# Two transformer blocks on one core: weight splits run further ahead, a late scaling moved, a bias moved from TensorE to VectorE, and a reordered latent head

## The chip, the cores and the metric

The kernel runs on one core of a Trainium2 chip, as one launch. The metric is the device time in microseconds (us), lower is better. The engines of the core that matter are TensorE (PE, matmuls; PEld is its weight load), VectorE (DVE), ScalarE (ACT), GpSimd (POOL) and the queue of SyncE (SP), which issues the transfers. Each engine has a list of instructions of its own; semaphores hold an instruction back until what it reads is there.

## The reference

Two blocks of two layers each work on 256 tokens of width 1024, in 32-bit floats. The first block (gated linear attention, a dense feed-forward and a mixture of eight experts) is not touched by the change. The second block has, for each of its two layers `i`, a feed-forward, an attention, a second feed-forward and a gated embedding:

```
for i in range(2):
    if i == 1: k_nope, k_rope, v = shared_kv(x, ...)
    x = post_norm(x, 0.5 * swiglu(x, ffn1_w_in[i], ffn1_w_out[i]), g0, b0)
    mix = fox_mixer(x, ...) if i == 0 else mla_mixer(x, ..., k_nope, k_rope, v)
    x = post_norm(x, mix, g1, b1)
    x = post_norm(x, 0.5 * swiglu(x, ffn2_w_in[i], ffn2_w_out[i]), g2, b2)
    gate = sigmoid(x @ ple_w_gate[i] + ple_b_gate[i])
    x = post_norm(x, gate * (p[i] @ ple_w_proj[i]), g3, b3)

swiglu(x)         = (silu(x @ w_gate) * (x @ w_up)) @ w_out      # 1024 -> 2816 -> 1024
post_norm(x, d)   = layer_norm(sqrt(2) * x + d) * g + b
mla_mixer: c_q    = rms_norm(x @ w_dq) * q_norm                   # 1024 -> 384, the "latent"
           q      = c_q @ w_uq ; keys and values from the shared latent of shared_kv
```

## The kernel before, in words

The 256 tokens are two tiles, t = 0 and 1, of 128 tokens (partitions) and 1024 columns. A product of 32-bit floats is made of three matmuls: each operand is split into a high part and a low part, and `mm3` (L304 to L311) adds high·high (L309), high·low and low·high (L310, L311) in one PSUM bank. The input of a stage is held turned round as `uh` and `ul` (high and low). The weights are split on the chip as well.

**The splitting of weights.** `want` queues the parts of the weights in the order in which they are used, a unit being a 128 x 2048 part of 1 MB that SP fetches into one of four `raw` buffers, and a half being 128 x 1024 of it. `emit(n)` splits the next n halves: a copy on ACT makes `wh` (L274), a subtraction on DVE makes `wl` (L275). At most `SLOTS` = 10 halves are live; a half gives its slot back when the last matmul that reads it has been written down, and a half of which a slot is not free is not begun. `tick(n)` calls `emit(n)` at fixed places of the program; where a stage has a string in the table `TICKS`, the digits of that string replace n until they are used up (the two first feed-forwards, `ffa0` and `ffa1`, have strings of 16 and 14 digits, the two second ones, `ffb0` and `ffb1`, none). `take(n)` hands units to a product and splits at once what is missing of them. The order in which instructions are written down is the order in which each engine runs them.

**The norm.** For each half of 512 columns, DVE adds the residual (`r`, L111) and takes statistics (L123); then `fin` makes `ve` (L331) on DVE and `rs` on POOL. `scale_all` makes x with two DVE operations per half (L149, L151); `apply` turns x round: eight PE transposes (L344), ACT writes `uh`, DVE `ul` (L361). The norm of tile 0 is done while the stage's last product of tile 1 runs. The two steps of tile 1 are put in the list `pend`; the next stage calls `nxt()` in the middle of its first products, and each call runs one of them.

**Feed-forward (`ffn`, L522).** The 2816 columns are 11 chunks j of 256. Chunks 0 and 1 go by token tile. From j = 2 on, `gate_up_T` (L449) makes two gates of 48 matmuls (i = 0, 1), each followed by ACT's `sg` (L468), DVE's `h` (L470) and the split of h in `fh` (ACT) and `fl` (DVE, L316), and by a product `down` of the chunk before (12 matmuls of 512 columns into `acc`). Each j uses six halves: four of gate and up, two of down. At the end come down(1, 9-1), down(0, 10), its norm, down(1, 9) and down(1, 10).

**Gated embedding (`ple`, L1747).** Four gates of 24 matmuls in the order (tile, half of columns) = (0,0), (0,1), (1,0), (1,1). The gate's bias is a row of 1024 numbers; it is fetched to one partition (`br`), split in `bh` and `bl`, and two matmuls with a contraction of one (L1775, L1776) add it to each gate in PSUM. Then ACT takes the sigmoid from PSUM, and DVE multiplies with the projection `pp` (L1792). `opened` runs in the middle of gate (0,0), `nxt` in the middle of gate (0,1).

**Latent attention (`mla`, L1546).** `down_q(t)` makes the latent of tile t (24 matmuls of 384 columns); its norm `cn` (L1480) goes over ACT, DVE and POOL, and then PE turns it round (L1487) and DVE and ACT split it (`cqh`, `cql`, L1492). `val` and `keys` make the values and keys of a pair of heads from the shared latent.

**Stages in the trace (us).** ffa0 about 1296 to 1512, forgetting attention (`fox`) 1516 to 1660, ffb0 1660 to 1852, ple0 1852 to 1894, shared_kv and ffa1 1894 to 2093, mla 2093 to 2270, ffb1 2270 to 2467, ple1 2467 to 2517. All before 1296 belongs to the first block.

Of the kernel before, what the change touches and what calls it, by code (L numbers as in the profile page):

```python
# [9 lines left out]
F32 = mybir.dt.float32  # L10
F32R = mybir.dt.float32r
BF16 = mybir.dt.bfloat16
AF = mybir.ActivationFunctionType
ALU = mybir.AluOpType
# [3 lines left out]
P = 128  # L18
D = 1024
S = 256  # L20
KB = D // P
# [26 lines left out]
ROW_LNB = 8  # L48
ROW_ADAG = 24
ROW_PLEB = 28  # L50
# [118 lines left out]
class Kern:  # L169
# [279 lines left out]
    def gate_up_T(self, wg, i, scale, pool, free, mid=None):  # L449

        nc = self.nc
        ps = self.pgu.tile([P, 512], F32, tag="gu", name="gu")
        for kb in range(KB):
            u, hf = wg[kb // 4], (kb % 4) // 2
            wh, wl = u.halves[hf]
            for g in range(2):
                o = (kb % 2) * 512 + g * CW + i * P

                self.mm3(ps[:, g * S:(g + 1) * S], wh[:, o:o + P], wl[:, o:o + P], self.uh[:, kb, :], self.ul[:, kb, :],
                         kb == 0 and g == 0, kb == KB - 1 and g == 1)  # L460
            if free and kb % 2:
                u.free(hf)
            if kb == 3:
                if mid:
                    mid()
                self.tick(self.rate)
        sg = self.acp.tile([P, CW], F32, name="sg")
        nc.scalar.activation(out=sg, in_=ps[:, :S], func=AF.Silu)  # L468
        h = self.acp.tile([P, S + 2], F32, tag="h", name="h")[:, :S]
        nc.vector.scalar_tensor_tensor(out=h, in0=sg, scalar=scale, in1=ps[:, S:], op0=ALU.mult, op1=ALU.mult)  # L470
        self.tick(self.rate)
        hh = pool.tile([P, S], F32R, name="fh", bufs=6)
        hl = pool.tile([P, S], F32R, name="fl", bufs=6)
        self.split(hh, hl, h)
        return hh, hl
# [46 lines left out]
    def ffn(self, name, scale, done, hook=None, early=None):  # L522


        wg, wd, h, hT, acc = {}, {}, {}, {}, {}
        n = NCH - 1

        def turn(s):
            hT[s] = self.parts_of(self.turn(h.pop(s)))

        def part(t, j):
            if j < 2:
                return hT.pop((t, j))
            return lambda i: tuple(z[:, t * P:(t + 1) * P] for z in hT[j, i])

        def down(t, j, norm=None, mid=None):
            if j not in wd:
                wd[j] = self.take()
            if j == 0:
                acc[t] = self.acc2()  # L540
            self.down(part(t, j), wd[j], acc[t], j == 0, j == n, t == 1, norm, mid)

        prev = None
        for i, (t, j) in enumerate([(0, 0), (0, 1), (1, 0), (1, 1)]):
            if hook and t == 0:
                hook(j)
            if i in (1, 2) and early:
                early(i)
            if j not in wg:
                wg[j] = self.take(2)  # L550

            def mid():
                if prev:
                    turn(prev)
                if i < 2:
                    self.nxt()
                if i == 0:
                    self.open_pool(name)
            ts = slice(t * P, t * P + P)
            h[t, j] = self.gate_up(lambda kb: self.uh[:, kb, ts], lambda kb: self.ul[:, kb, ts], wg[j], scale, t == 1,  # L560
                                   mid)
            if prev:
                down(*prev)
            prev = t, j
        for j in range(2, n + 1):
            if hook:
                hook(j)
            wg[j] = self.take(2)
            for i in range(2):
                first = (j, i) == (2, 0)  # L570
                hT[j, i] = self.gate_up_T(wg[j], i, scale, self.mp, i == 1, (lambda: turn(prev)) if first else None)
                if first:
                    down(*prev)

                elif j > 2 and not (i == 1 and j >= n - 1):
                    down(i, j - 1)
        down(1, n - 2)
        n0, n1 = done(0, acc[0]), done(1, acc[1])
        down(0, n, n0)
        n0.scale_all()  # L580
        down(1, n - 1)
        down(1, n, n1, n0.apply)
        self.close_pool()
        self.pend.extend([n1.scale_all, n1.apply])


    def proj_tok(self, ps, t, units, kbs=range(KB), free=False, mid=None, width=512, last=True):

        ts = slice(t * P, t * P + P)
        for kb in kbs:  # L590
            u, hf = units[kb // 4], (kb % 4) // 2
            wh, wl = u.halves[hf]
            sl = slice((kb % 2) * width, (kb % 2) * width + width)
            self.mm3(ps[:, :width], self.uh[:, kb, ts], self.ul[:, kb, ts], wh[:, sl], wl[:, sl], kb == 0,
                     last and kb == KB - 1)
            if free and kb % 2:
                u.free(hf)
            if kb == 3 and mid:
                mid()
            if kb % (2 if free else 4) == (1 if free else 3):  # L600
                self.tick()
# [238 lines left out]
    def out_rest(self, uo, y, kbs, done, acc):  # L840
        n0 = done(0, acc)
        n0.stats()
        n0.scale_all()
        acc = self.acc2()
        self.out_proj(uo, y(1), acc, kbs, True, True, True, {4: n0.apply}, 5)
        n1 = done(1, acc)
        n1.stats()
        self.pend.extend([n1.scale_all, n1.apply])

    def gla_turn(self, kout, st):  # L850

# [694 lines left out]
    def mla(self, done, row):  # L1546
        nc, tc, a = self.nc, self.tc, self.a
        scale = 192.0 ** -0.5
        c = {}
# [17 lines left out]
        def down_q(t, mid=None):  # L1567
            ps = self.pgu.tile([P, 512], F32, tag="gu", name="gu")
            self.proj_tok(ps, t, ud, free=t == 1, width=384, mid=mid)
            return self.rms_T(ps[:, :384], 384, COL_QN, c["cqh"], c["cql"], t)  # L1570
# [109 lines left out]
        self.nxt()  # L1680
        kn[0] = keys(kv)
        self.tick(0)
        kv, us[1] = self.take(2)
        v[1] = val(kv)
        f0()
        self.tick(0)
        f1 = down_q(1)
        self.rows(row)
        kn[1] = keys(kv)
        self.tick(0)  # L1690
        f1()
        qr[0], rest = rope(uq)
        qn[0] = queries(uq)
        rest()
# [40 lines left out]
                n0.apply()  # L1735
        n1 = done(1, acc[1])
        n1.stats()
        self.pend.extend([n1.scale_all, n1.apply])
        self.close_pool()


# [5 lines left out]
    def ple(self, i, done, row):  # L1747
        nc, a = self.nc, self.a
        c = {}

        def opened():
            self.nxt()
            self.open_pool(f"ple{i}")
            mp = self.mp
            pT = mp.tile([P, 2 * S], F32, name="pT")
            nc.sync.dma_start(out=pT, in_=a["ple_p"][i])
            ph = c["ph"] = mp.tile([P, 2 * S], F32R, name="ph")
            pl = c["pl"] = mp.tile([P, 2 * S], F32R, name="pl")
            self.split(ph, pl, pT)
            br = mp.tile([1, D], F32, tag="delta", bufs=2, name="br")  # L1760
            nc.sync.dma_start(out=br, in_=a["rows"][ROW_PLEB + i:ROW_PLEB + i + 1, :])
            bh = c["bh"] = mp.tile([1, D], F32R, name="bh")
            bl = c["bl"] = mp.tile([1, D], F32R, name="bl")
            self.split(bh, bl, br)
            one = c["one"] = mp.tile([1, P], F32R, name="one")
            nc.scalar.copy(one, self.onesf[:1, :])

        ug = self.take(4)
        d = {}

        def gate(t, hf, mid=None):
            ps = self.pgu.tile([P, 512], F32, tag="gu", name="gu")
            self.proj_tok(ps, t, ug[2 * hf:2 * hf + 2], free=t == 1, mid=mid, last=False)
            sl = slice(hf * 512, hf * 512 + 512)
            nc.tensor.matmul(ps, c["one"], c["bh"][:, sl], start=False, stop=False)  # L1775
            nc.tensor.matmul(ps, c["one"], c["bl"][:, sl], start=False, stop=True)  # L1776
            if t not in d:
                d[t] = self.mp.tile([P, D], F32, tag="delta", name="delta", bufs=2)
            nc.scalar.activation(out=d[t][:, sl], in_=ps, func=AF.Sigmoid)

        def emb(t, hf):
            sl = slice(hf * 512, hf * 512 + 512)
# [23 lines left out]
        for hf in range(2):  # L1806
# [4 lines left out]
            times(1, hf, pp[hf])  # L1811
            norms[1].stat(hf)
        norms[1].fin()
        self.close_pool()
        self.pend.extend([norms[1].scale_all, norms[1].apply])


    def load_ahead(self, *tiles):
# [196 lines left out]
    def second(self, layers=range(2)):  # L2015
        def norm(i, mode="T"):
            return lambda t, ps: Norm(self, t, ps, None, mode=mode)

        def rows_at(i):
            return lambda j: self.rows(ROW_LNB + 2 * i) if j == 3 else None  # L2020
        for l in layers:
# [17 lines left out]
            if self.stop == n + 1:  # L2039
                return self.dump()  # L2040
            self.phase(f"ffb{l}")
            self.ffn(f"ffb{l}", 0.5, norm(i + 2), rows_at(i + 2))
            if self.stop == n + 2:
                return self.dump()
            self.phase(f"ple{l}")
# [141 lines left out]
```

## Time and profile before

| what | value |
| --- | --- |
| time, median of 3 runs | 2522.14 us (2520.14 to 2528.19) |
| profiled execution: time, span | 2518.69 us, 2517.0 us |
| mean granted TensorE clock | 0.982 |
| PE busy | 2401.0 us (95%) |
| DVE busy | 1795.2 us (71%) |
| ACT busy | 1306.9 us (52%) |
| POOL busy | 46.7 us (2%) |
| DMA, mean | 238 GB/s |

PE is busy for 95% of the span, so that all its idle time is 116 us. A row of the timeline gives the start, the length, the engine, the line, the operation, what it writes and reads, and in brackets the idle time before it on its engine with the instruction that ended it. A matmul's length as shown overlaps the next one; the distance of two starts tells what one costs. PEclk is the clock that TensorE was granted, as a share of its 2.4 GHz level.

### The profile page before, as it was taken

To read this page: it belongs to the slowest core of one execution; us is meant where nothing else is said; L and a number is where in the kernel's file an instruction comes from. 1 tells how busy PE (TensorE), PEld (TensorE's weight loads), DVE (VectorE), ACT (ScalarE), POOL (GpSimd) and SP (SyncE) were. 2 spreads that over 40 slices of the span, in tenths; PEclk is the share of its full clock that TensorE was granted. 3 is DMA by queue.
4 is the path that set the end of the run, shared out by engine and by line. 5 is a ranking of instruction groups with operands and counts; after the bars stand their busy time and mean duration, and the time that the engine had idled before them with its cause. 6 is when DMAs were issued, how large, how long until landed. Compare 5 with 4: busy or idle time off the path is not lost. (4 is left out here: it accounts for less than half of the span.)

```text
span 2517.0 us, 34411 instructions
## 1 busy us (share of the span) xinstructions
PE 2401.0 (95%) x13608; PEld 2018.2 (80%) x13608; DVE 1795.2 (71%) x2587; ACT 1306.9 (52%) x1949; POOL 46.7 (2%) x79
## 2 busy tenths in 40 slices
PE   8999989899999999999979999999989998999997
PEld 5769978588788888888858887879968997878995
DVE  6876886699899999999984456655476556546546
ACT  3344443287777777777743345534434444443432
POOL 0000000000000000000000000000000001000000
PEclk9999999899999999999989999999999999999998
DMA  9756957479899999999855444335545544334551
GB/s 357 296 201 256 355 209 287 151 269 370 325 356 367 344 347 373 348 348 363 339 227 197 176 164 170 116 141 190 188 172 190 183 173 155 113 117 152 184 201 55
DMA packets 88925, 599.45 MB, mean 238 GB/s; under 512 B 10259, under 2 KB 11571, under 8 KB 20533
## 3 DMA queue, kind: packets, MB, share of 16 engines
q1 hardware_dynamic: 88756, 597.19, 63.3%
q8 instruction: 108, 1.77, 0.3%
q14 instruction: 61, 0.49, 0.1%
HBM read 596.10 MB, written 1.05 MB: 237 GB/s over the span
## 5 line engine op out<-in xcount | busy, mean ns | idle before, releaser
L275 DVE TENSOR_TENSOR wl<-raw,wh 128x1024 fp32r<-128x1024 f32 (+3 forms) x997 | 1162.4, 1208 | 124.5 <-ACT wh L274 120.1
L274 ACT CAST wh<-raw 128x1024 fp32r<-128x1024 f32 (+3 forms) x997 | 987.2, 1040 | 78.9 <-DMA raw<-in_moe_gu_dram 18.9
L309 PE MATMUL gu<-uh,wh 128*128 128x256 f32 (+1 forms) x1784 | 504.3, 283 | 0.6 <-ACT cc L784 0.6
L311 PE MATMUL gu<-uh,wl 128*128 128x256 f32 (+1 forms) x1784 | 501.5, 281 | 3.1 <-DVE wl L275 3.1
L310 PE MATMUL gu<-ul,wh 128*128 128x256 f32 (+1 forms) x1784 | 500.5, 281 | 0.0
L309 PEld LDWEIGHTS gu<-uh,wh 128*128 128x128 f32 (+1 forms) x1784 | 335.1, 188 | 6.8 <-issue 1.2
L310 PEld LDWEIGHTS gu<-ul,wh 128*128 128x128 f32 (+1 forms) x1784 | 335.3, 188 | 4.5 <-issue 0.3
L311 PEld LDWEIGHTS gu<-uh,wl 128*128 128x128 f32 (+1 forms) x1784 | 335.7, 188 | 3.8 <-DVE wl L275 3.3
L309 PE MATMUL gu<-wh,xs 128*128 128x512 f32 x704 | 280.8, 399 | 0.6 <-PEq L1285 0.6
L311 PE MATMUL gu<-wh,xs 128*128 128x512 f32 x704 | 277.2, 394 | 0.0
L310 PE MATMUL gu<-wl,xs 128*128 128x512 f32 x704 | 276.2, 392 | 0.0
L468 ACT ACTIVATE sg<-gu 128x256 f32<-128x256 f32 x90 | 34.7, 385 | 404.8 <-PE gu L311 404.8
L470 DVE SCALAR_TENSOR_TENSOR h<-sg,gu 128x256 f32<-128x256 f32 x90 | 37.9, 421 | 279.5 <-ACT sg L468 279.5
L310 PE MATMUL acc<-wl,hh 128*128 128x512 f32 x432 | 171.2, 396 | 2.6 <-DVE wl L275 2.6
L311 PE MATMUL acc<-wh,hl 128*128 128x512 f32 x432 | 170.5, 395 | 1.7 <-DVE hl L316 1.6
L309 PE MATMUL acc<-wh,hh 128*128 128x512 f32 x432 | 170.9, 396 | 0.5 <-ACT hh L315 0.5
L311 PEld LDWEIGHTS gu<-wh,xs 128*128 128x128 f32 x704 | 132.3, 188 | 29.4
L309 PEld LDWEIGHTS gu<-wh,xs 128*128 128x128 f32 x704 | 132.5, 188 | 26.7 <-DVE h L445 1.0
L310 PEld LDWEIGHTS gu<-wl,xs 128*128 128x128 f32 x704 | 132.6, 188 | 26.3
L310 PE MATMUL acc<-wl,fh 128*128 128x512 f32 x360 | 142.7, 396 | 8.3 <-DVE wl L275 8.3
L309 PE MATMUL acc<-wh,fh 128*128 128x512 f32 x360 | 144.0, 400 | 1.0
L315 ACT CAST hh<-trh 128x256 fp32r<-128x256 f32 x108 | 40.3, 373 | 195.9 <-PE trh L481 195.8
(394 smaller groups left out, 3399.3 us busy)
## 6 DMA issues: line engine op xcount, KB each, us to landing
raw<-in_moe_gu_dram SPq DMA_DIRECT2D x175, 1024.0 KB, 5.5
raw<-in_ffn_gu_dram SPq DMA_DIRECT2D x110, 1024.0 KB, 4.8
raw<-in_moe_dn_dram SPq DMA_DIRECT2D x87, 1024.0 KB, 5.0
raw<-in_ffn_dn_dram SPq DMA_DIRECT2D x55, 1024.0 KB, 4.9
raw<-in_ada_w_dram SPq DMA_DIRECT2D x48, 1024.0 KB, 5.1
raw<-in_w_in_dram SPq DMA_DIRECT2D x24, 1024.0 KB, 5.9
raw<-in_fox_in_dram SPq DMA_DIRECT2D x12, 1024.0 KB, 5.1
ww<-in_w_out_dram SPq DMA_DIRECT2D x16, 512.0 KB, 7.9
```

What stands on the lines that cost most here:

```text
L274: nc.scalar.copy(wh[:, :f], r)
L275: nc.vector.tensor_tensor(out=wl[:, :f], in0=r, in1=wh[:, :f].bitcast(F32), op=ALU.subtract)
L309: mm(out, xh, yh, start=first, stop=False)
L310: mm(out, xh, yl, start=False, stop=False)
L311: mm(out, xl, yh, start=False, stop=last)
L315: self.nc.scalar.copy(h, src)
L468: nc.scalar.activation(out=sg, in_=ps[:, :S], func=AF.Silu)
L470: nc.vector.scalar_tensor_tensor(out=h, in0=sg, scalar=scale, in1=ps[:, S:], op0=ALU.mult, op1=ALU.mult)
```

## The change

Five edits. (1) In `gate_up_T` both calls of `tick` offer two halves instead of one (`self.rate` is 1 in the second block and 2 in the first). (2) The scaling of tile 1, `n1.scale_all`, is written at the end of its own stage instead of in the next one's first product; `None` keeps its place in `pend`. This is done in `ffn`, `out_rest` (the end of the linear and the forgetting attention), `mla` and `ple`. (3) The bias of the gated embedding is fetched as 128 equal rows (`pleb`, 512 KB) in chunk 4 of the feed-forward before it; DVE adds it to the gate from PSUM into `delta`, and ACT takes the sigmoid in place. The two matmuls per gate, the split of the bias row and its transfer are gone. (4) The rows of the norm are still fetched at chunk 3, by the new hook. (5) In `mla` the second tile's latent product `down_q(1)` comes before `val(1)` instead of behind it, and the second turn (`f1`) comes before `keys(1)` instead of behind it.

```diff
--- before.py
+++ after.py
@@ -463,12 +463,12 @@
             if kb == 3:
                 if mid:
                     mid()
-                self.tick(self.rate)
+                self.tick(2)
         sg = self.acp.tile([P, CW], F32, name="sg")
         nc.scalar.activation(out=sg, in_=ps[:, :S], func=AF.Silu)
         h = self.acp.tile([P, S + 2], F32, tag="h", name="h")[:, :S]
         nc.vector.scalar_tensor_tensor(out=h, in0=sg, scalar=scale, in1=ps[:, S:], op0=ALU.mult, op1=ALU.mult)
-        self.tick(self.rate)
+        self.tick(2)
         hh = pool.tile([P, S], F32R, name="fh", bufs=6)
         hl = pool.tile([P, S], F32R, name="fl", bufs=6)
         self.split(hh, hl, h)
@@ -580,11 +580,12 @@
         n0.scale_all()
         down(1, n - 1)
         down(1, n, n1, n0.apply)
+        n1.scale_all()
         self.close_pool()
-        self.pend.extend([n1.scale_all, n1.apply])
-
-
-    def proj_tok(self, ps, t, units, kbs=range(KB), free=False, mid=None, width=512, last=True):
+        self.pend.extend([None, n1.apply])
+
+
+    def proj_tok(self, ps, t, units, kbs=range(KB), free=False, mid=None, width=512):
 
         ts = slice(t * P, t * P + P)
         for kb in kbs:
@@ -592,7 +593,7 @@
             wh, wl = u.halves[hf]
             sl = slice((kb % 2) * width, (kb % 2) * width + width)
             self.mm3(ps[:, :width], self.uh[:, kb, ts], self.ul[:, kb, ts], wh[:, sl], wl[:, sl], kb == 0,
-                     last and kb == KB - 1)
+                     kb == KB - 1)
             if free and kb % 2:
                 u.free(hf)
             if kb == 3 and mid:
@@ -845,7 +846,8 @@
         self.out_proj(uo, y(1), acc, kbs, True, True, True, {4: n0.apply}, 5)
         n1 = done(1, acc)
         n1.stats()
-        self.pend.extend([n1.scale_all, n1.apply])
+        n1.scale_all()
+        self.pend.extend([None, n1.apply])
 
     def gla_turn(self, kout, st):
 
@@ -1680,15 +1682,15 @@
         self.nxt()
         kn[0] = keys(kv)
         self.tick(0)
+        f1 = down_q(1)
+        f0()
+        self.rows(row)
         kv, us[1] = self.take(2)
         v[1] = val(kv)
-        f0()
         self.tick(0)
-        f1 = down_q(1)
-        self.rows(row)
+        f1()
         kn[1] = keys(kv)
         self.tick(0)
-        f1()
         qr[0], rest = rope(uq)
         qn[0] = queries(uq)
         rest()
@@ -1735,7 +1737,8 @@
                 n0.apply()
         n1 = done(1, acc[1])
         n1.stats()
-        self.pend.extend([n1.scale_all, n1.apply])
+        n1.scale_all()
+        self.pend.extend([None, n1.apply])
         self.close_pool()
 
 
@@ -1757,26 +1760,18 @@
             ph = c["ph"] = mp.tile([P, 2 * S], F32R, name="ph")
             pl = c["pl"] = mp.tile([P, 2 * S], F32R, name="pl")
             self.split(ph, pl, pT)
-            br = mp.tile([1, D], F32, tag="delta", bufs=2, name="br")
-            nc.sync.dma_start(out=br, in_=a["rows"][ROW_PLEB + i:ROW_PLEB + i + 1, :])
-            bh = c["bh"] = mp.tile([1, D], F32R, name="bh")
-            bl = c["bl"] = mp.tile([1, D], F32R, name="bl")
-            self.split(bh, bl, br)
-            one = c["one"] = mp.tile([1, P], F32R, name="one")
-            nc.scalar.copy(one, self.onesf[:1, :])
 
         ug = self.take(4)
         d = {}
 
         def gate(t, hf, mid=None):
             ps = self.pgu.tile([P, 512], F32, tag="gu", name="gu")
-            self.proj_tok(ps, t, ug[2 * hf:2 * hf + 2], free=t == 1, mid=mid, last=False)
+            self.proj_tok(ps, t, ug[2 * hf:2 * hf + 2], free=t == 1, mid=mid)
             sl = slice(hf * 512, hf * 512 + 512)
-            nc.tensor.matmul(ps, c["one"], c["bh"][:, sl], start=False, stop=False)
-            nc.tensor.matmul(ps, c["one"], c["bl"][:, sl], start=False, stop=True)
             if t not in d:
                 d[t] = self.mp.tile([P, D], F32, tag="delta", name="delta", bufs=2)
-            nc.scalar.activation(out=d[t][:, sl], in_=ps, func=AF.Sigmoid)
+            nc.vector.tensor_tensor(out=d[t][:, sl], in0=ps, in1=self.pleb[:, sl], op=ALU.add)
+            nc.scalar.activation(out=d[t][:, sl], in_=d[t][:, sl], func=AF.Sigmoid)
 
         def emb(t, hf):
             sl = slice(hf * 512, hf * 512 + 512)
@@ -1811,8 +1806,9 @@
             times(1, hf, pp[hf])
             norms[1].stat(hf)
         norms[1].fin()
+        norms[1].scale_all()
         self.close_pool()
-        self.pend.extend([norms[1].scale_all, norms[1].apply])
+        self.pend.extend([None, norms[1].apply])
 
 
     def load_ahead(self, *tiles):
@@ -2039,7 +2035,14 @@
             if self.stop == n + 1:
                 return self.dump()
             self.phase(f"ffb{l}")
-            self.ffn(f"ffb{l}", 0.5, norm(i + 2), rows_at(i + 2))
+            def hook(j):
+                if j == 3:
+                    self.rows(ROW_LNB + 2 * (i + 2))
+                if j == 4:
+                    self.pleb = self.rowp.tile([P, D], F32, tag="grow", name="pleb")
+                    self.nc.sync.dma_start(out=self.pleb,
+                                           in_=self.a["rows"][ROW_PLEB + l:ROW_PLEB + l + 1, :].to_broadcast([P, D]))
+            self.ffn(f"ffb{l}", 0.5, norm(i + 2), hook)
             if self.stop == n + 2:
                 return self.dump()
             self.phase(f"ple{l}")
```

The next rows are DVE's in the loop of ffa0, from a gate's `h` on, before. `wl` is the low part of a weight half, `h` and `fl` are the gate's result and its low part.

```order
L470 SCALAR_TENSOR_TENSOR h<-sg,gu 128x256
L275 TENSOR_TENSOR wl<-raw,wh 128x1024
L316 TENSOR_TENSOR fl<-h,fh 128x256
L275 TENSOR_TENSOR wl<-raw,wh 128x1024 x2
L470 SCALAR_TENSOR_TENSOR h<-sg,gu 128x256
```

The same place after the change:

```order
L470 SCALAR_TENSOR_TENSOR h<-sg,gu 128x256
L275 TENSOR_TENSOR wl<-raw,wh 128x1024 x2
L316 TENSOR_TENSOR fl<-h,fh 128x256
L275 TENSOR_TENSOR wl<-raw,wh 128x1024 x2
L470 SCALAR_TENSOR_TENSOR h<-sg,gu 128x256
L316 TENSOR_TENSOR fl<-h,fh 128x256
L275 TENSOR_TENSOR wl<-raw,wh 128x1024 x2
```

Two `wl` now stand between `h` and `fl` of one gate of the chunk (the second, i = 1), none in the other's; before, each gate had one there.

DVE from the end of ffb0 into ple0, before: `ve` is the last step of tile 1's statistics, `r` and `x` are its scaling, `pl` the low part of the embedding, `bl` that of the bias, `ul` the turned tile, and `delta<-pp,delta` the product with the gate.

```order
L331 TENSOR_SCALAR ve<-mv 128x1
L275 TENSOR_TENSOR wl<-raw,wh 128x1024 x4
L149 SCALAR_TENSOR_TENSOR r<-r,mv,G 128x512 x2
L151 SCALAR_TENSOR_TENSOR x<-r,rs,B 128x512 x2
L316 TENSOR_TENSOR pl<-pT,ph 128x512
L316 TENSOR_TENSOR bl<-br,bh 1x1024
L275 TENSOR_TENSOR wl<-raw,wh 128x1024 x2
L361 TENSOR_TENSOR ul<-pt,uh 128x4x128 x2
L1792 TENSOR_TENSOR delta<-pp,delta 128x512 x2
```

After:

```order
L331 TENSOR_SCALAR ve<-mv 128x1
L275 TENSOR_TENSOR wl<-raw,wh 128x1024
L149 SCALAR_TENSOR_TENSOR r<-r,mv,G 128x512 x2
L151 SCALAR_TENSOR_TENSOR x<-r,rs,B 128x512 x2
L316 TENSOR_TENSOR pl<-pT,ph 128x512
L1773 TENSOR_TENSOR delta<-gu,pleb 128x512
L361 TENSOR_TENSOR ul<-pt,uh 128x4x128 x2
L1773 TENSOR_TENSOR delta<-gu,pleb 128x512
L1787 TENSOR_TENSOR delta<-pp,delta 128x512 x2
```

The scaling moved from behind four `wl` to behind one, `bl` went, and an addition from `gu` stands behind `pl` and another behind `ul`.

DVE in ple0 between tile 0's statistics and its turn, after the change (before, the row with `pleb` is not there):

```order
L128 BN_AGGR mv<-st 128x2
L331 TENSOR_SCALAR ve<-mv 128x1
L275 TENSOR_TENSOR wl<-raw,wh 128x640 x4
L1773 TENSOR_TENSOR delta<-gu,pleb 128x512
L149 SCALAR_TENSOR_TENSOR r<-r,mv,G 128x512 x2
L151 SCALAR_TENSOR_TENSOR x<-r,rs,B 128x512 x2
L361 TENSOR_TENSOR ul<-pt,uh 128x4x128 x2
L1787 TENSOR_TENSOR delta<-pp,delta 128x512
```

The addition for gate (1,0) now stands ahead of tile 0's scaling.

DVE at the head of mla, before; `ms`, `ve` and `cn` are the norm of the latent, `cqh` and `cql` its turned parts:

```order
L1478 TENSOR_SCALAR ms<-ms 128x1
L331 TENSOR_SCALAR ve<-ms 128x1
L1480 TENSOR_SCALAR cn<-gu,rs 128x384
L275 TENSOR_TENSOR wl<-raw,wh 128x768
L275 TENSOR_TENSOR wl<-raw,wh 128x384
L361 TENSOR_TENSOR ul<-pt,uh 128x4x128 x2
L275 TENSOR_TENSOR wl<-raw,wh 128x1024
L1492 CAST cqh<-cf 128x3x128
L1493 TENSOR_TENSOR cql<-cf,cqh 128x3x128
L275 TENSOR_TENSOR wl<-raw,wh 128x1024 x2
L1478 TENSOR_SCALAR ms<-ms 128x1
```

After:

```order
L1480 TENSOR_SCALAR ms<-ms 128x1
L331 TENSOR_SCALAR ve<-ms 128x1
L1482 TENSOR_SCALAR cn<-gu,rs 128x384
L361 TENSOR_TENSOR ul<-pt,uh 128x4x128 x2
L275 TENSOR_TENSOR wl<-raw,wh 128x1024 x3
L275 TENSOR_TENSOR wl<-raw,wh 128x768
L1480 TENSOR_SCALAR ms<-ms 128x1
L331 TENSOR_SCALAR ve<-ms 128x1
L1482 TENSOR_SCALAR cn<-gu,rs 128x384
L1494 CAST cqh<-cf 128x3x128
L1495 TENSOR_TENSOR cql<-cf,cqh 128x3x128
```

Both `cn` now come ahead of both `cqh`, and the `wl` that stood between the first `ms` and its `cqh` come behind `ul`.

## Rows read from the trace of the kernel before

**Rows 1.** The page's head.

```profile
span 2517.0 us, 34411 instructions
```

**Rows 2.** PE's waits from 1290 to the end: total us, times, longest.

```profile
PE gu L1776 <- DVE bl L316: 10.9, 2, 5.5
PE acc L310 <- DVE wl L275: 10.2, 14, 0.8
```

**Rows 3.** Timeline of PE in ple0: start, length, instruction, idle before it.

```profile
1857.72 0.39 PE L311 MATMUL gu<-wh,ul 128*128 128x512 f32 x1
1864.00 0.79 PE L1776 MATMUL gu<-bl,one 1*128 1x512 f32 x1 [5.46 <-DVE bl L316]
1864.72 0.80 PE L309 MATMUL gu<-wh,uh 128*128 128x512 f32 x1
...
1869.05 0.39 PE L310 MATMUL gu<-wl,uh 128*128 128x512 f32 x1
...
1872.95 0.39 PE L311 MATMUL gu<-wh,ul 128*128 128x512 f32 x1
...
1873.93 0.50 PE L309 MATMUL pp<-wh,ph 128*128 128x512 f32 x1
```

**Rows 4.** Window in ple0: PE, PEld, DVE, ACT, POOL busy, then PEclk.

```profile
1864.00:1866.00 2.00, 2.00 (x4) 1.37 (x5) 2.00 (x2) 0.60 (x1) 0.00 (x0) 0.50 0.90 222
```

**Rows 5.** Timeline of DVE in ple0.

```profile
1854.94 4.63 DVE L275 TENSOR_TENSOR wl<-raw,wh 128x1024 fp32r<-128x1024 f32 x4
...
1862.74 1.21 DVE L316 TENSOR_TENSOR bl<-br,bh 1x1024 fp32r<-1x1024 f32 x1
```

**Rows 6.** Timeline of PE in the feed-forward loops.

```profile
1369.52 0.50 PE L310 MATMUL acc<-wl,fh 128*128 128x512 f32 x1 [0.76 <-DVE wl L275]
...
1386.00 0.39 PE L311 MATMUL acc<-wh,fl 128*128 128x512 f32 x1
...
1387.74 0.50 PE L310 MATMUL acc<-wl,fh 128*128 128x512 f32 x1 [0.76 <-DVE wl L275]
1388.08 0.40 PE L311 MATMUL acc<-wh,fl 128*128 128x512 f32 x1
...
2446.07 0.50 PE L310 MATMUL acc<-wl,fh 128*128 128x512 f32 x1 [0.76 <-DVE wl L275]
```

**Rows 7.** Timeline of PE and DVE around gate (1,0) of ple0.

```profile
1875.19 0.39 PE L311 MATMUL pp<-wh,pl 128*128 128x512 f32 x1
...
1875.62 0.69 DVE L1792 TENSOR_TENSOR delta<-pp,delta 128x512 f32<-128x512 f32 x1 [3.57 <-PE pp L311]
...
1884.04 1.41 DVE L149 SCALAR_TENSOR_TENSOR r<-r,mv,G 128x512 f32<-128x512 f32 x2
...
1884.91 0.40 PE L311 MATMUL gu<-wh,ul 128*128 128x512 f32 x1
...
1886.26 1.29 PE L344 MATMUL pt<-ident,x 128*128 128x128 f32 x8 [0.29 <-DVE x L151]
```

**Rows 8.** Timeline of PE at the start of ffa0.

```profile
1313.02 1.94 PE L344 MATMUL pt<-ident,x 128*128 128x128 f32 x8 [2.57 <-DVE x L151]
```

**Rows 9.** Timeline of DVE and PE at the end of ffb0.

```profile
1840.98 0.42 DVE L316 TENSOR_TENSOR fl<-h,fh 128x256 fp32r<-128x256 f32 x1
...
1842.15 0.39 PE L311 MATMUL acc<-wh,fl 128*128 128x512 f32 x1
```

**Rows 10.** Timeline of PE at the start of fox.

```profile
1524.76 1.29 PE L344 MATMUL pt<-ident,x 128*128 128x128 f32 x8 [0.80 <-DVE x L151]
```

**Rows 11.** Timeline of PE at the head of mla.

```profile
2103.60 0.39 PE L309 MATMUL gu<-wh,ck 128*128 128x256 f32 x1 [1.04 <-DVE cn L1480]
...
2112.71 0.55 PE L1487 MATMUL pt<-ident,cn 128*128 128x128 f32 x3 [0.96 <-DVE cn L1480]
...
2114.87 0.58 PE L309 MATMUL gu<-cqh,wh 128*128 128x256 f32 x1 [1.61 <-DVE cqh L1492]
```

**Rows 12.** Window in the mixture of experts, columns as in Rows 4.

```profile
700.00:800.00 100.00, 100.00 (x455) 81.62 (x454) 94.45 (x105) 75.40 (x98) 0.00 (x0) 1.00 0.95 364
```

## The prediction

> **What bounds the kernel now.** I read the page's head and the busy times first: PE works for 2401.0 of the 2517.0 us of the span [rows 1], so the time is a full PE plus the places where it stands still, and an edit is worth what it does to those. Next I read PE's waits from 1290 us on, where the changed code begins to act: two waits for the bias's low part, 10.9 us together, and fourteen for `wl` in the down products, 10.2 us [rows 2]. Then the timeline around each wait. In ple0 the reader sees the first gate end, a stop of 5.46 us, and matmuls that start 0.42 us apart behind it [rows 3], at a granted clock of 0.50 [rows 4]. In the loops he sees the same stop of 0.76 us again and again [rows 6]. The step of a 512-column matmul at full clock is (1884.91 − 1875.19) / 42 = 0.231 us [rows 7]; all costs below are distances of starts minus such steps. Terms are against the profiled execution, 2518.69 us (span 2517.0 [rows 1] and 1.7 around it), 3.4 below the median of the runs shown, 2522.14.
>
> **Bias on VectorE (gain 19.1).** The second bias matmul of gate (0,0) stands behind `bl`, and `bl` runs at 1862.74 although its gate ends at 1858.1, because four `wl` (4.63 us), `r`, `x` and `pl` stand ahead of it on DVE by the order, and four `wl` alone take that long [rows 5]. From the gate's last own matmul to the next gate's first are 7.00 us where 0.23 would do: 6.77 [rows 3]. The ten matmuls behind take 4.33 us in place of 2.31, at half clock: 2.02 [rows 3, 4]. Gate (0,1) loses 0.98 − 0.23 = 0.75 to its two bias matmuls [rows 3]. Sum 9.5. The second wait, in ple1, is as long (10.9 for two [rows 2]), so 2 × 9.5 = 19.1. The other two gates per stage also lose their matmuls (0.75 each), but at the end of the stage DVE is what PE or the output waits for, and there an addition from PSUM, as long as the product `delta<-pp,delta` at 0.69 [rows 7], takes the place of 0.75: nothing, within 0.3. On the first two gates the addition runs beside the next gate's 24 matmuls (5.5 us). Gate (0,1) has the other of two PSUM buffers, so it waits for none of this. What is late next there: the turn of tile 1 in the middle of gate (0,1), some 2.8 us after gate (0,0) ends; its `x` now stands behind one `wl`, not four, and is there by 1857. The 512 KB of equal rows are fetched 100 us before use; if they came late, the first sigmoid would, and gate (1,0) would wait for its PSUM buffer. Lower end of this term: half of it stays (9.5), as some other DVE work holds the first gates.
>
> **The wait that it adds (loss 3.2).** In ple0 the addition for gate (1,0) stands on DVE ahead of the scaling of tile 0, whose turn PE wants right behind that gate. Before, `r` started at 1884.04, 0.87 us before that gate's last matmul, and PE resumed with the turn at 1886.26, 2.22 after `r` and 1.35 after that matmul [rows 7]. Now the addition begins 0.43 after the last matmul (as `delta<-pp,delta` at 1875.62 follows 1875.19), lasts 0.69, and `r` follows at 1.15; the turn comes at 1.15 + 2.22 = 3.37. That is 2.02 later, and queued behind `r` are `x`, `ul` and so all of gate (1,1). PE stands still for nearly 3 us; after a stop of 2.57 us the eight transposes took 1.94 [rows 8] against 1.29 [rows 7], so I add 0.65 and half a microsecond for the next matmuls: 3.2 (2.0 to 3.3; the far end 5.5, the stop in rows 3, if the half clock lasts as long as there). In ple1 there is no turn. The Trainium skill states, on the page "PSUM — Partial Sum Buffer", section "Engine vs sequencer instructions", that VectorE's queue is strictly first in, first out. Rows 5 agree: `bl` ran in the written place, long after its gate had ended. If the engine could take `r` ahead of the addition, this term would be zero and the sum 3.2 larger (2484.8).
>
> **Splits up to ten ahead (gain 13.9).** In the loop the stop of 0.76 us comes once per chunk: 1386.00 to 1388.08 is 2.08 us for three steps, 0.69, so 1.39 each [rows 6]. There are ten that the edit reaches: eight in ffa0, of which the first two stand in rows 6, 18.22 us apart, one in ffb0 and one in ffb1 (the last row). The other four of the fourteen lie at heads of stages or before 1296 and stay. Ten halves are offered per chunk and six used, so that a few chunks after the start all live slots are filled, a chunk ahead; the stop comes from a down half split just before its use. Ten times 1.39 is 13.9. The DVE has room: six `wl` at 1.16 [rows 5] and two each of `h` and `fl` at 0.42 [rows 9] are 8.6 us of 18.22. Low end 5 (the strings of ffa0 still feed its start), high end 16.
>
> **The ends of the feed-forwards (loss 3.9).** In the order the second gate of a chunk has two `wl` between `h` and `fl`, where it had one, and so has the last gate of all. Before, `fl` started at 1840.98 and PE wanted it at 1842.15 [rows 9]. One more `wl` (1.16) puts its end at 1842.56, 0.4 late, with about 0.3 for the restart; tile 0's norm behind it is 0.5 late at the stage's last turn: 1.2 in ffa0, ffb0 and ffb1, 0.3 in ffa1, 3.9. Bounds: none, if these `wl` were done in the loop, and 3 × (1.16 + 1.39) = 7.7 if each stops PE as in rows 6.
>
> **Scaling at its stage's end (gain 1.5).** At the start of fox tile 1's turn waits 0.80 [rows 10], since `x` stands behind four `wl`; now behind one. A stop of 0.76 cost 1.39 above, so 1.5. The ends of the other stages have no such wait or no new order; 0 to 2.2.
>
> **Latent head (gain 3.3).** `keys(0)` waits 1.04 for a PSUM buffer that `cn` frees, and the first queries wait 1.61 for `cqh` [rows 11]. `cn` now has no `wl` ahead, and between the second turn and the queries there is `keys(1)`. Those two go, 2.65, and some 0.6 of restarts; the 0.96 before the second turn stays, since the norm of the latent lasts longer than `val(1)`. Bounds −2 (the turns wait twice as long) and 5.
>
> **Sum.** 19.1 − 3.2 + 13.9 − 3.9 + 1.5 + 3.3 = 30.7; 2518.7 − 30.7 = 2488.0. By the median of the runs it would be 2491.4; I say 2490.
>
> **Rivals.** (a) Casts ahead of results, slower: a split that waits for a slot stands ahead of `h` and `fl` in DVE's list; if its wait outlasts its gate, the down product is one `wl` late, 1.2 us, in each of the 36 second gates of the four loops: 43 lost, 2518.7 − 30.7 + 43 = 2531. It decides once the slots free later than the gate ends. For it: two `wl` do stand behind the `h` of these gates. Against: the experts' stage feeds the same way with DVE at 94.45 of 100 us and PE at 100.00 [rows 12], and slots come free while a gate runs. (b) The loop's stops stay because the raw part is late, not DVE: 13.9 less, 2501.9. Against: the releaser is DVE each time [rows 6]. (c) The stop in the gated embedding comes back as a wait behind `pl` or the additions, half of 19.1 and the larger end of the added wait: 2488.0 + 9.5 + 2.3 = 2500. For it: DVE's list there is still long. (d) The feed-forward ends and the latent head come out at their good ends, and the loops at theirs: 2488.0 − 3.9 − 1.7 − 2.1 = 2480. (e) The edit does nothing of weight, since slots bind the splits and other waits follow: 2515 to 2522.
>
> **How the numbers follow.** Forecast (2483 to 2496) 0.55; (b) 0.10, (c) 0.13, (d) 0.13, (a) 0.04, (e) 0.05. From 2478 to 2504 these hold all but the 0.09 of (a) and (e) and the tails of the others, near 0.8. What a measurement can tell from no change is 0.3%, 7.6 us. Faster by more than that: the forecast, (b), (c), (d), 0.91 and a little of (e), 0.92. Within it: most of (e), 0.05. Slower: 0.03, the worse part of (a).
>
> **What will show it.** Right: in ple0 and ple1 no PE wait between the first two gates and clock 1.0 there; no wait of 0.76 in the loops after 1369; `h` and `fl` ended before PE asks; in ple0 a PE stop of 2.5 to 3 us after gate (1,0), ended by `x`, that was 0.29; at the ends of ffa0, ffb0 and ffb1 a PE wait for `fl`; the first turn of fox without its 0.80. Wrong: PE waits for `fl` or `h` in the middle of a loop (a), `wl` waits that stay with a transfer as the releaser (b), PE waiting for a PSUM buffer in the gated embedding (c), or a span above 2505.

## The result and the profile after

The changed kernel takes 2487.86 us in the median of 4 runs (2482.52 to 2493.80), the kernel before 2524.47; the ratio is 0.9859, with a 95% interval from 0.9841 to 0.9877. The forecast was 2490, faster. The profiled execution's span fell from 2517.0 to 2486.0 us. Run once more beside other variants and on another chip (`a_again` below), the same kernel's ratio was 0.9873, some 32 us, where 35 to 36 were expected.

The page's head and, in a second view, PE's waits from 1290 on (line waited for: total us, times, longest), which answer to [rows 1, 2]:

```profile
span 2486.0 us, 34474 instructions
```

```profile
PE acc L310 <- DVE wl L275: 2.6, 4, 0.8
...
PE acc L311 <- DVE fl L316: 0.9, 3, 0.3
```

The waits for `bl` are gone, four of the fourteen for `wl` are left (the four that lie outside the loops), and three short waits for `fl` are new.

To see where the time went, I cut the second part at the turns (the eight transposes that turn one tile's `x` round, which every kernel has at the same place of its program) and compare the lengths. The cut begins at tile 1's turn in ffa0: 1313.02 before [rows 8] and, after:

```profile
1314.34 1.94 PE L344 MATMUL pt<-ident,x 128*128 128x128 f32 x8 [2.46 <-DVE x L151]
```

| from turn to turn | before | after | difference | predicted |
| --- | --- | --- | --- | --- |
| ffa0, to its tile 0's turn | 199.04 | 188.79 | −10.25 | −11.1 + 1.2 |
| to the turn of tile 1 in fox | 12.70 | 11.00 | −1.70 | −1.5 |
| fox and the head of ffb0 | 141.54 | 141.16 | −0.38 | 0 |
| ffb0, to its tile 0's turn | 182.70 | 182.23 | −0.47 | −1.4 + 1.2 |
| ple0, to its tile 0's turn | 37.26 | 29.54 | −7.72 | −9.5 + 2.0 |
| rest of ple0, shared_kv, ffa1 | 204.56 | 207.06 | +2.50 | +1.2 + 0.3 |
| mla, to tile 0's turn | 178.68 | 174.62 | −4.06 | −3.3 |
| ffb1, from there to its tile 0's turn | 194.26 | 193.76 | −0.50 | −1.4 + 1.2 |
| ple1, to the end | 53.24 | 43.50 | −9.74 | −9.5 |
| sum | 1203.98 | 1171.66 | −32.32 | −30.6 |

The added wait's 3.2 stands here as 2.0 before tile 0's turn in ple0 and 1.2 behind it. Place by place the sum holds within 1.1 us. PE in ple0 after, the answer to [rows 3, 4] (the end of gate (0,0) and the start of gate (0,1)), and the window around it (PE, PEld, DVE, ACT, POOL busy, PEclk):

```profile
1846.01 0.39 PE L310 MATMUL gu<-wl,uh 128*128 128x512 f32 x1
1846.23 0.40 PE L311 MATMUL gu<-wh,ul 128*128 128x512 f32 x1
1846.47 0.39 PE L309 MATMUL gu<-wh,uh 128*128 128x512 f32 x1
```

```profile
1846.20:1848.20 2.00, 2.00 (x10) 1.60 (x9) 2.00 (x4) 0.00 (x0) 0.00 (x0) 1.00 0.56 209
```

Starts stand 0.23 apart throughout, at the full clock (1.00). The wait that the change adds, the answer to [rows 7]: DVE and PE around gate (1,0), and the clock behind it.

```profile
1863.80 0.40 PE L311 MATMUL gu<-wh,ul 128*128 128x512 f32 x1
...
1864.24 0.69 DVE L1773 TENSOR_TENSOR delta<-gu,pleb 128x512 f32<-128x512 f32 x1 [1.22 <-PE gu L311]
1864.84 1.41 DVE L149 SCALAR_TENSOR_TENSOR r<-r,mv,G 128x512 f32<-128x512 f32 x2
...
1867.06 0.64 PE L344 MATMUL pt<-ident,x 128*128 128x128 f32 x2 [2.86 <-DVE x L151]
```

```profile
1867.10:1869.10 2.00, 2.00 (x9) 2.00 (x10) 0.80 (x2) 0.67 (x2) 0.00 (x0) 0.50 0.34 143
```

The turn begins 3.26 behind the gate's last matmul; 3.37 was predicted. The clock is at its lower level (0.50) behind the stop, as supposed. In the loop of ffa0 the down product now runs without a gap, three steps of 0.23 where [rows 6] had 2.08:

```profile
1386.01 0.39 PE L311 MATMUL acc<-wh,fl 128*128 128x512 f32 x1
1386.24 0.39 PE L309 MATMUL acc<-wh,fh 128*128 128x512 f32 x1
1386.46 0.39 PE L310 MATMUL acc<-wl,fh 128*128 128x512 f32 x1
1386.70 0.39 PE L311 MATMUL acc<-wh,fl 128*128 128x512 f32 x1
```

The end of ffa0 [rows 9 show ffb0's before], the turn in fox [rows 10] and the head of mla [rows 11]:

```profile
1495.80 0.50 PE L311 MATMUL acc<-wh,fl 128*128 128x512 f32 x1 [0.31 <-DVE fl L316]
1503.13 1.05 PE L344 MATMUL pt<-ident,x 128*128 128x128 f32 x5 [1.29 <-DVE x L151]
...
1514.13 1.03 PE L344 MATMUL pt<-ident,x 128*128 128x128 f32 x8
...
2093.10 0.55 PE L1489 MATMUL pt<-ident,cn 128*128 128x128 f32 x3 [1.66 <-DVE cn L1482]
```

`fl` is 0.31 late (0.28 in ffb0 and ffb1), the wait for `x` before the turn at the end of ffa0 is 1.29 where it was 0.92, the turn of fox has no wait, and of mla's waits one is left, for `cn`, longer than each that went.

### The profile page after: what moved, and what is told of

It reads as the page before. It is cut to its first block, busy times and chain, and to the rows that moved or that the text cites. A ratio compares the mean times of both kernels' runs of the same rounds, so it can differ in the third digit from the quotient of the medians.

```text
span 2486.0 us, 34474 instructions
## 1 busy us (share of the span) xinstructions
PE 2386.9 (96%) x13592; PEld 2016.7 (81%) x13592; DVE 1802.7 (73%) x2593; ACT 1314.6 (53%) x1945; POOL 44.6 (2%) x79
## 5 line engine op out<-in xcount | busy, mean ns | idle before, releaser
L311 PE MATMUL acc<-wh,fl 128*128 128x512 f32 x360 | 141.8, 394 | 1.2 <-DVE fl L316 1.2
```

Source lines behind the costliest of these rows:

```text
L311: mm(out, xl, yh, start=False, stop=last)
```

## The experiments

Each edit was made alone on the kernel before (names with b_) and undone alone in the changed kernel (a_); three more change the order further. The lengths of the second part (from tile 1's turn in ffa0 to the end) and of the stretches of the table above are from the profiles, one of each kernel. Each ratio is against the kernel before as it was run beside that variant, so it is not the quotient of two medians of this table.

| kernel | median us | ratio to before, interval | second part | ffa0 to fox's turn | ple0 | mla | ple1 |
| --- | --- | --- | --- | --- | --- | --- | --- |
| before | 2524.47 | | 1203.98 | 211.74 | 37.26 | 178.68 | 53.24 |
| changed | 2487.86 | 0.9859, 0.9841 to 0.9877 | 1171.66 | 199.79 | 29.54 | 174.62 | 43.50 |
| a_again | 2493.24 | 0.9873, 0.9851 to 0.9896 | 1171.67 | 199.86 | 29.54 | 174.50 | 43.43 |
| b_ticks_only | 2502.90 | 0.9917, 0.9904 to 0.9931 | 1183.89 | 199.93 | 33.19 | 179.25 | 49.37 |
| b_bias_only | 2515.45 | 0.9965, 0.9952 to 0.9979 | 1200.99 | 214.63 | 30.84 | 184.13 | 46.63 |
| b_head_only | 2522.54 | 1.0001, 0.9985 to 1.0016 | 1203.98 | 211.95 | 37.56 | 177.20 | 53.92 |
| b_scale_only | 2522.58 | 1.0001, 0.9989 to 1.0012 | 1205.81 | 213.23 | 37.61 | 178.84 | 53.37 |
| a_ticks_back | 2505.88 | 0.9939, 0.9918 to 0.9959 | 1189.67 | 211.53 | 30.07 | 178.50 | 46.63 |
| a_bias_back | 2497.72 | 0.9900, 0.9885 to 0.9915 | 1180.99 | 199.93 | 33.20 | 176.19 | 49.31 |
| a_head_back | 2493.80 | 0.9886, 0.9862 to 0.9909 | 1179.01 | 201.50 | 29.64 | 181.78 | 43.57 |
| a_scale_first | 2486.11 | 0.9849, 0.9826 to 0.9872 | 1164.96 | 199.73 | 26.63 | 174.62 | 43.46 |
| a_end | 2505.84 | 0.9924, 0.9901 to 0.9947 | 1187.07 | 202.45 | 33.45 | 182.35 | 47.23 |
| a_end2 | 2482.16 | 0.9845, 0.9829 to 0.9861 | 1166.40 | 198.54 | 29.48 | 176.02 | 43.43 |
| best3 | 2480.70 | 0.9835, 0.9817 to 0.9853 | 1161.91 | 197.16 | 26.55 | 177.22 | 43.36 |

The changed kernel's second part came out the same in two profiles (1171.66, 1171.67), but lowered clock still moves single stretches. Behind its stop for `xr` (the rotated part of the queries), mla has the same matmuls in the same order in the kernel before, b_bias_only, the changed kernel, a_head_back and a_end; up to tile 0's turn they take 143.29 and 148.33, and 143.68, 148.25 and 148.34, at mean clocks of 1.00 and 0.94, and 0.99, 0.94 and 0.94. So some 4.6 of a difference in mla can be the clock's alone. Variants of the changed kernel whose intervals overlap are told apart by such stretches only, not by the times.

**b_ticks_only.** Two lines of the kernel before:

```diff
-                self.tick(self.rate)
+                self.tick(2)
-        self.tick(self.rate)
+        self.tick(2)
```

> The kernel before with the ticks of two alone. Theory 1 (the terms of the prediction add up edit by edit): 13.9 gained in the loops, 3.9 lost at the ends, 10.0 faster than before; in ple0 and ple1 PE still stops 5.5 us for the bias's low part. Theory 2 (the edits overlap: more halves ahead also take three of the four wl from in front of the scaling and of the bias's low part): that stop falls by 3 x 1.16 = 3.5 to about 2.0 us in each of the two stages and the half clock behind it goes (2 x 5.5), and the wait of 0.80 in fox goes (1.5): 22 to 23 faster.

20 faster, theory 2 but for the clock. The bias is still on PE, but the stop is 2.04. PE's waits for it, and the timeline of DVE and PE in ple0:

```profile
PE gu L1776 <- DVE bl L316: 4.1, 2, 2.0
```

```profile
1844.44 1.22 DVE L275 TENSOR_TENSOR wl<-raw,wh 128x1024 fp32r<-128x1024 f32 x1
1845.57 1.41 DVE L149 SCALAR_TENSOR_TENSOR r<-r,mv,G 128x512 f32<-128x512 f32 x2
...
1848.82 1.20 DVE L316 TENSOR_TENSOR bl<-br,bh 1x1024 fp32r<-1x1024 f32 x1
...
1850.08 0.49 PE L1776 MATMUL gu<-bl,one 1*128 1x512 f32 x1 [2.04 <-DVE bl L316]
```

One `wl` stands where four did, here and ahead of fox's scaling, since the halves that ple0 needs were split in the loop. ple0 and ple1 gain 4.1 and 3.9 by this alone, and fox's turn its 1.7. The clock behind the stop still falls: it is 0.69 from 1850.5 to 1852.5, and ten matmuls take 3.88 (1850.84 to 1854.72) where 2.31 would do.

**b_bias_only.** The kernel before with the row `pleb`, the addition and the sigmoid in place, as in the diff of the change.

> The kernel before with the bias on VectorE alone. Theory 1: 2 x 9.5 gained, 3.2 lost by the addition ahead of tile 0's scaling, 16 faster. Theory 2: the scaling of tile 1 still stands behind four wl, x is there at about 1862.3 of the profile before, and its turn in the middle of the second gate is wanted at 1860.7: a stop of 1.5 us stays in each of the two stages; 12 to 13 faster.

9 faster by the ratio, short of both. ple0 and ple1 gain 6.4 and 6.6. The stop for `x` that theory 2 names is there in both stages, 0.79 and not 1.5; what else was late behind `bl` shows in ple1, where the projection's halves end PE's waits too:

```profile
2480.18 1.29 PE L344 MATMUL pt<-ident,x 128*128 128x128 f32 x8 [0.79 <-DVE x L151]
2485.66 0.50 PE L309 MATMUL pp<-wh,ph 128*128 128x512 f32 x1 [0.70 <-ACT wh L274]
2486.92 0.50 PE L310 MATMUL pp<-wl,ph 128*128 128x512 f32 x1 [0.76 <-DVE wl L275]
```

The rest of the shortfall lies in stretches that the edit does not touch (ffa0 2.9 longer, mla 5.5), where its clock is lower: 0.98 and not 0.99 over ffa0, and in mla as above.

**a_bias_back.** The same lines reversed in the changed kernel.

> The changed kernel with the bias given back to TensorE (row fetched to one partition, split, two matmuls per gate), the other edits kept. Theory 1: 15.9 slower than the changed kernel (19.1 less 3.2). Theory 2: the bias's low part stands behind one wl and not four, the stop is 2.0 us without a lowered clock, 2 x (2.0 + 0.75) lost and the 3.2 of the added wait regained: 2 to 5 slower than the changed kernel, 33 faster than the kernel before.

9.3 of the second part, between the two: 3.7 in ple0 and 5.8 in ple1, 1.6 in mla (no matmul of mla differs; its clock is 0.98 and not 0.99), less 1.9 that come back behind ple0. Theory 2 had the stop right:

```profile
PE gu L1779 <- DVE bl L316: 4.1, 2, 2.0
```

It had the clock wrong: behind the same stop b_ticks_only loses 1.6 in ple0 to it (3.88 against 2.31, above), for which I had put nothing. What else makes up the 5.8 in ple1 is not taken apart.

**a_ticks_back.** The two lines of b_ticks_only reversed.

> The changed kernel with the ticks of one again, the other edits kept. Theory 1: 10.0 slower than the changed kernel; ten PE waits of 0.76 for wl are back in the loops. Theory 2: the same 10 in the feed-forwards, and up to 3 more at the head of mla, where cn again stands behind wl; the gated embedding keeps its gain since the bias is not on TensorE: 10 to 13 slower.

18.0 of the second part, more than either theory. The loop of ffa0 and fox's turn return 11.7 of it, mla loses 3.9, and ple1 3.1, with waits of 1.37 and 0.76 for the projection's halves, which neither theory had.

**a_head_back** (the order in mla reversed) and **b_head_only** (made alone):

```diff
-        f1 = down_q(1)
-        f0()
-        self.rows(row)
         kv, us[1] = self.take(2)
         v[1] = val(kv)
+        f0()
         self.tick(0)
+        f1 = down_q(1)
+        self.rows(row)
```

and `f1()` behind `keys(1)` again.

> The changed kernel with the old order at the head of mla. Theory 1 (the new order hides the norm of the latent behind other products): 3.3 to 5 slower than the changed kernel; the PE waits for cn (1.0) and cqh (1.6) are back. Rival (with the splits done earlier there is no wl ahead of cn in either order, so the order is worth nothing): within 1 of the changed kernel.

> The kernel before with the new order at the head of mla alone. Theory 1 (the norm of the latent is hidden behind other products, whatever the splits): 3 to 4 faster than the kernel before in the stretch from ffa0 on. Rival (with few halves ahead the wl before cn keep it late, so the order alone is worth less): 0 to 1.5 faster.

In the changed kernel the old order makes mla 7.2 longer, with the stop for `cqh` (1.61) back and that for `xr` longer (1.80 for 1.49), with a clock of 0.50 behind it; the interval of the times (0.9886 against 0.9873) can't tell it from zero. Nor is all of it the order's. Cut at the start of the first matmul behind the stop for `xr`, into head and rest (length, then PE, PEld, DVE, ACT, POOL busy, PEclk), the changed kernel and then a_head_back show:

```profile
2074.12:2105.06 30.94, 26.54 (x172) 23.49 (x172) 20.80 (x41) 15.46 (x35) 4.13 (x7) 1.00 0.36 117
2105.06:2248.74 143.68, 136.32 (x818) 111.40 (x819) 76.89 (x173) 68.56 (x160) 0.91 (x1) 0.99 0.34 119
...
2074.86:2108.39 33.53, 28.01 (x173) 24.98 (x173) 20.45 (x40) 15.15 (x34) 4.12 (x7) 0.94 0.31 106
2108.39:2256.64 148.25, 142.16 (x819) 115.59 (x820) 77.42 (x173) 68.96 (x161) 0.91 (x1) 0.94 0.32 116
```

The order is worth 2.6 in the head; the other 4.6 lie behind it, where the matmuls are the same and the clock is lower. By the same cut the head takes 35.39 in the kernel before, 33.54 with the new order alone, 33.51 with the ticks alone and 30.94 with all edits. Alone the order shortens mla by 1.5 and the second part by nothing, as the rival said: with few halves ahead, two `wl` stand ahead of the norm of the latent, and PE waits 1.13 for `cn` and 1.25 for `ul`.

**b_scale_only.** `n1.scale_all()` at the stage's end, alone.

> The kernel before with the scaling of the second tile at its stage's end alone. Theory 1 (the prediction: fox's wait of 0.80 goes, nothing else): 1.5 faster. Rival (the low part of the bias still stands behind the same wl, pl and scaling, so ple0 and ple1 stay; the moved scaling puts three wl behind it that the next stage wants): 0.5 faster to 1 slower.

Nothing, as the rival said. Fox's wait of 0.80 does go, but one of 0.26 for `wl` comes just ahead of the turn, and the stretch up to there gains 0.4 (12.28 against 12.70), where the ticks gain 1.7. The opposite, the changed kernel without this edit, need not be run: its instructions on every engine are in the same order, since with the splits done in the loop nothing is left to be written between the two places. So this edit does nothing in the changed kernel, and what I gave it in fox belongs to the ticks.

**a_scale_first.** One line in `ple`, ahead of gate (1,0), in the changed kernel:

```diff
+        norms[0].scale_all()
         for hf in range(2):
             gate(1, hf)
```

> The changed kernel with tile 0's scaling in ple0 written ahead of gate (1,0), so that the addition of that gate stands behind it and not ahead. Theory 1 (the prediction's added wait of 3.2): the PE stop of 2.86 us in ple0 shrinks to 0.3 or less and the transposes behind it run at full clock; 3 to 3.5 faster than the changed kernel. Rival: the scaling delays the four wl of 640 columns behind it by 2.8 us, and shared_kv's products wait for them instead: no faster than 1.

ple0 is 2.9 shorter; the turn follows its gate without a stop, and what follows it up to mla gains another 0.9:

```profile
1858.59 1.41 DVE L151 SCALAR_TENSOR_TENSOR x<-r,rs,B 128x512 f32<-128x512 f32 x2
1859.92 3.02 DVE L275 TENSOR_TENSOR wl<-raw,wh 128x640 fp32r<-128x640 f32 x4
...
1861.71 1.03 PE L344 MATMUL pt<-ident,x 128*128 128x128 f32 x8
...
1862.86 0.68 DVE L1773 TENSOR_TENSOR delta<-gu,pleb 128x512 f32<-128x512 f32 x1
```

3.8 for the wait that was put at 3.2. The rival is there too, but small: PE's wait for `wl` in the next product is 3.40 where it was 2.69. (Another 2.9 of its second part lies in fox, where no instruction differs and the clock is 1.00 and not 0.98.) The addition ahead of the scaling was the cause, not the bias's place.

**a_end and a_end2.** In both, the last gate's second tick is left out; a_end offers two halves behind tile 0's scaling, a_end2 also leaves out the tick in tile 0's statistics and offers three behind tile 1's scaling. In the diff, cut to its lines of effect, `end` marks the last gate, the added `tick` is a_end's, and the `emit` a_end2's; a_end does this in the first block's feed-forward too, ahead of the second part:

```diff
-        self.tick(2)
+        if not end:
+            self.tick(2)
         n0.scale_all()
+        self.tick(2)
         down(1, n - 1)
         down(1, n, n1, n0.apply)
         n1.scale_all()
+        self.emit(3)
```

> The changed kernel with no splits between the last gate's h and fl of a feed-forward; two are offered behind tile 0's scaling instead. Theory 1 (the prediction's 3.9 at the ends, and the wait for x it was added to): the PE waits for fl (0.3) and for x (1.3, 1.3, 0.9, 1.3) before the turn go; 6 to 8 faster than the changed kernel. Rival: the two wl only move, and stand ahead of ul and of tile 1's statistics, so that the next stage's first product waits up to 2.3 longer for ul: between 2 slower and 2 faster.

> The changed kernel with no splits on DVE between the last gate's h and fl and none between tile 0's statistics and its scaling; three halves are offered behind tile 1's scaling instead, where a_end had two ahead of ul. Theory 1 (at the ends DVE's order is all that counts): the PE waits for fl (0.3) and x (1.3, 1.3, 0.9, 1.3) before the turns go and ul stays as in the changed kernel; 6 to 8 faster than it. Rival (these halves are wanted at once by the next stage): the waits go but PE stops for wl in the first product of fox, mla, ple0 and ple1; between 2 slower and 3 faster.

a_end is 15.4 slower than the changed kernel in the second part, worse than its rival. `fl` is in time, and the wait for `x` falls to 0.9 or less, but three `wl` stand ahead of `ul` at each end, and PE waits 1.8 to 2.8 for `ul` there, where it was 0.5 or less. Of the 15.4, 4.7 lie in mla behind its head, in the clock, as above. The timeline at the end of ffb0, and the window behind it (columns as above):

```profile
1845.24 3.48 DVE L275 TENSOR_TENSOR wl<-raw,wh 128x1024 fp32r<-128x1024 f32 x3
1848.65 0.68 DVE L111 SCALAR_TENSOR_TENSOR r<-x,acc 128x512 f32<-128x512 f32 x1
...
1849.97 1.27 DVE L361 TENSOR_TENSOR ul<-pt,uh 128x512 fp32r<-128x512 f32 x2
1850.70 0.50 PE L311 MATMUL gu<-wh,ul 128*128 128x512 f32 x1 [2.75 <-DVE ul L361]
```

```profile
1852.00:1854.00 2.00, 2.00 (x6) 1.54 (x5) 1.93 (x4) 0.19 (x1) 0.86 (x1) 0.51 0.03 8
```

a_end2, with such work placed behind everything that PE waits for in its own stage, is 5.3 faster than the changed kernel in its second part, a little less than theory 1's 6 to 8: 2.0 in each of ffa0, ffb0 and ffb1 and 1.4 up to ffa1's end, while 0.7 is lost in front of fox's turn and 1.4 in mla, where the three `wl` stand ahead of the latent's norm. So theory 1 is right about the ends, which cost what they cost by DVE's order, and the rival has those 2.1.

**best3.** Both edits together.

> a_end2 and a_scale_first together: the gains of both, 3.6 and that of a_end2, since they lie in different stretches; 9 to 11 faster than the changed kernel by theory 1, 2 to 6 by the rival of a_end2.

9.8 less than the changed kernel in the second part, and 0.9835 of the kernel before; the intervals of the two (0.9817 to 0.9853, 0.9851 to 0.9896 for a_again) just touch. Its two halves do not separate from the changed kernel by their times, only by the stretches.

## Why the prediction was right

**The places** were right: each stop named in the trace of before went, for about its price, and the new ones (the turn behind gate (1,0), `fl` at the ends) came as predicted; the sum is 30.7 against 32.3 of the second part, and the runs' medians differ by 36.6 (28.6 beside a_again), which the spread of the runs covers: in these profiles tile 1's turn in ffa0, with the same program ahead of it, starts anywhere from 1313.0 to 1319.8.

**The shares by edit** were wrong in one step, which the sum hides: "Bias on VectorE (gain 19.1)". I charged the whole stop behind `bl`, four `wl` included, to the edit that removes `bl`, and counted the ticks only in the loops. Alone, the ticks give 20.1 and the bias 3.0 by the second part (9 by the times), not 10.0 and 15.9; with the others present they give 18.0 and 9.3. Three of the four `wl` ahead of `bl`, and three of the four ahead of fox's scaling, are the ticks' doing; the 1.5 put down to the scaling at its stage's end is theirs too. The sum came out all the same because it counts each place once, whichever edit gets the price. The order of the change showed one `wl` there, and I read it as a fact of ple0 and not of the loop. The four edits alone shorten the second part by 21.3 (with the clock's 8 us in b_bias_only, about 29), all together by 32.3. They are not independent at the places (ple0: ticks 4.1 and bias 6.4 do not add, 7.7 with all edits; ple1: 3.9 and 6.6, 9.7 with all). In the head of mla they nearly add: 1.9 by the ticks, 1.9 by the order, 4.45 with all; over the whole of mla the clock hides it.

**The added wait** was put at 3.2 and measured at 3.8 by taking it away. **The ends** were put at 3.9, 1.2 for each of three; the waits that came there are 0.3 for `fl` and 0.4 more for `x` (1.29 for 0.92). Taking the `wl` away from the ends gains 7.3 (2.1 lost elsewhere), because the wait of 0.92 for `x` was there before already. **The latent head** was put at 3.3, for the order, and the stretch shows 4.1; but the order is worth 2.6 with the ticks and 1.9 without, and the rest is the ticks', which take `wl` from ahead of `cn`. Of the rivals, (a) did not happen: no PE wait for `h` or `fl` in a loop; (b) did not: the `wl` waits went with the ticks alone; (c) did not in the changed kernel; b_bias_only has waits of 0.7 to 0.8 in the gated embedding, for `x` and for the projection's halves.

The strict order of VectorE's queue, which the Trainium skill states ("PSUM — Partial Sum Buffer", "Engine vs sequencer instructions"), is borne out here. In the changed kernel DVE stands idle for 1.22 until gate (1,0) ends, with the addition next in its list and the scaling behind it; in a_scale_first the two stand in the other order, and the stop of 2.86 is gone.

## What to carry to other kernels

Where a wait ends behind a queue of work on another engine, split its price over what stands in that queue, and give each part to the edit that moves it; the edit that removes the last instruction in the queue gets only its own part. Look-ahead work on an in-order engine belongs behind the last instruction that someone waits for in its stage: splits at the ends cost 15 us ahead of `ul` (4.7 of it perhaps not theirs) and gained 5 behind the scaling. An edit that moves code past nothing moves no instruction; the list of instructions shows it without a run.

## What was not expected of the hardware

The clock behind a stop is not told by the stop's length alone. At one place of mla, with the same matmuls behind it, a stop of 1.82 (2126.21, before) was followed by a granted clock of 1.00, and one of 1.83 in b_bias_only by 0.50; 1.49 in the changed kernel was followed by 1.00, and 1.51 in a_end by 0.50. In ple0, 2.04 in b_ticks_only was followed by 0.69 from 1850.5 to 1852.5. Such stretches add up to some 5 us in one stage (mla, 178.68 before against 184.13 in b_bias_only), as much as the smaller edits are worth. What decides it is left open.

The sigmoid of 128x512 in place took 0.63 from SBUF (1864.96, changed kernel) and 0.60 from PSUM (1864.83, before), and so, within 0.01, did all eight of either kernel: 0.03 more for the side that it reads.
